# Own raw buffers for the weight steps with sums, and attention tables loaded once per layer

## The chip, the cores and the metric

The kernel runs on one core of a Trainium2 chip. The metric is the device time of one execution in microseconds (us), lower is better. The engines are named as in the profile: PE is TensorE (matrix products; PEld is its loading of weights), DVE is VectorE, ACT is ScalarE, POOL is GpSimd, and SP is SyncE, which here only issues transfers (DMAs).

## The reference

A two-layer encoder in float32 over 256 positions of width 2048. Cut to what matters:

```python
for l in range(2):
    h = rms_norm(x, attn_norm[l])
    proj = h @ w_in[l]
    ...
    mixed = jnp.concatenate([out_a, out_b, out_c], axis=-1)
    x = x + mixed @ w_o[l]
    h = rms_norm(x, mlp_norm[l])
    x = x + jnp.square(jax.nn.relu(h @ w_up[l])) @ w_down[l]
return rms_norm(x, final_norm)
```

`w_up[l]` is 2048x8192 and `w_down[l]` 8192x2048. The three mixers `out_a`, `out_b`, `out_c` are attention of three kinds; they need tables that do not depend on the input (cosines and sines of the rotary part, a mask, distances).

## The kernel before, in words

**Weights in two parts.** PE multiplies in a format with fewer bits than float32, so each weight tile is split: ACT casts the loaded raw tile to a high part (`wh`, line 132 or 147) and DVE subtracts that from the raw tile for a low part (`wl`, line 133 or 148). Activations are split in the same way, and each product is three matmuls (high by high, high by low, low by high).

**Stages.** A prologue loads `x` and the first weights and makes the statistic of the first norm: squares on POOL, line 252, added up in `acc`, line 253. Then comes, per layer, an attention phase and an MLP phase, which use the same region of on-chip memory one after the other: a pool is opened with the phase, `here["pool"]`. Other pools hold for the whole program: `cp` (x, gains, the tables `cn`, which are 128x1408 and hold the 128x128 identity `ident` in their first 128 columns, and others), `wp` (weights), `tp` (small work tiles, among them the rings `t1k` and `s2k` of three buffers each).

**MLP.** A layer's MLP takes four quarters of the hidden width; each quarter has two up products (names u00, u01, u10, ... quarter and half) and two down products (d00, d01, ...), so a layer has 16 products, and the program 32. `Product` (lines 281 to 353) computes one. It has 8 steps. A step loads two raw halves of 128x1024 (512 KB each, line 310, on SP's queue) and splits them. Steps 1, 2, 4, 5 and 7 are **plain**: two `wh`, two `wl`, 24 matmuls of 128x512. Steps 0, 3 and 6 are **steps with sums**: they save matmuls by working with sums of blocks of the weight. DVE forms the sums in place in the raw halves (lines 324 to 327), and these are split a second time into `th` and `tl` (ACT and DVE, two buffers each in the phase's pool). So a raw half of a plain step is free after its `wl`, one of a step with sums only after its `tl`: the second half (`raw[1]`) after the `tl` with the ending _2, the first (`raw[0]`) after that with the ending _3. After step 6 the results are put together on DVE (lines 346 to 350, `c`), after step 7 the last addition follows (line 352). An up product then goes through relu (ACT, line 771) and 16 transposes on PE (line 361) to a square (line 775); a down product's results are transposed and added to `x` by DVE (line 791).

All weights of the kernel, of plain steps and of steps with sums, go through one ring of four raw buffers:

```python
def rawt(name):
    return wp.tile([P, HW], F32, tag="raw", name=name, bufs=4)
```

`wh` and `wl` have five buffers each. A transfer into a buffer is issued when what the buffer held has been read for the last time. SP issues in the order that the program has for it, so an issue that waits holds up all behind it.

**What sets the order.** The framework simulates the program when it is built and orders each engine's instructions; tiles get their buffers in that order. There are no due times by hand.

The tables are loaded once, in the prologue, by `load_consts` (lines 119 to 121): `cn` and then `lm`, the vectors of the learned lambda, of which DVE makes `lamp` and `lams` (lines 442 to 449).

Of the kernel before, what the change touches and what calls it, by code (L numbers as in the profile page):

```python
# [10 lines left out]
F32 = mybir.dt.float32  # L11
# [5 lines left out]
P = 128  # L17
D = 2048
T = 256
DEPTH = 2  # L20
# [8 lines left out]
HW = 1024  # L29
# [7 lines left out]
def hybrid_encoder(ctx: ExitStack, tc: tile.TileContext, xT, wA, wQ, wKV, wB, wC, wO, wU, wD,  # L37
# [25 lines left out]
        return next(units(name, shape))  # L63

    def t1k(name):
        return tp.tile([P, T], F32, tag="t1k", name=name, bufs=3)

    def s2k(name):
        return tp.tile([P, 2, T], F32, tag="s2k", name=name, bufs=3)
# [31 lines left out]
    xp = [cp.tile([P, 2, T], F32, tag=f"x{k}", name=f"x{k}") for k in range(KT // 2)]  # L101
    x = [xp[k // 2][:, k % 2, :] for k in range(KT)]
    gn = cp.tile([P, G_END], F32, tag="gn", name="gn")
    cn = cp.tile([P, C_END], F32, tag="cn", name="cn")
    lm = tp.tile([P, DEPTH * 4 * 64], F32, tag="s2k", name="lm", bufs=3)
    ones = cp.tile([P, P], F32, tag="ones", name="ones")
    mhalf = cp.tile([P, 8], F32, tag="mhalf", name="mhalf")
# [2 lines left out]
    nc.gpsimd.memset(mhalf, -0.5)  # L110
    ones_r = cp.tile([P, P], F32R, tag="ones_r", name="ones_r")
    nc.scalar.copy(ones_r, ones)
    ident = cn[:, C_ID:C_ID + P]
    cosT = cn[:, C_COS:C_COS + T]
    sinT = cn[:, C_SIN:C_SIN + T]
    maskA = cn[:, C_MASK:C_MASK + 384]
    dist = cn[:, C_DIST:C_DIST + 384]

    def load_consts():
        nc.sync.dma_start(cn, consts)  # L120
        nc.sync.dma_start(lm, lams.to_broadcast([P, DEPTH * 4 * 64]))


    def weights(src, name, steps=(HW, HW)):
# [109 lines left out]
    class Stat:  # L234
# [7 lines left out]
        def add(self, xt):  # L242
            self.n += 1
            if self.n == 1:
                nc.gpsimd.tensor_tensor(self.acc, xt, xt, op=ALU.mult)  # L245
                return
            s = t1k(f"sq_{self.name}_{self.n}")
            if self.n == KT:
                nc.scalar.activation(s, xt, AF.Square)
                self.last = [s]  # L250
            else:
                nc.gpsimd.tensor_tensor(s, xt, xt, op=ALU.mult)
                nc.gpsimd.tensor_tensor(self.acc, self.acc, s, op=ALU.add)
# [27 lines left out]
    class Product:  # L281
# [22 lines left out]
        def step(self, i):  # L304
            nm = f"{self.name}_{i}"
            a = self.acts[i]
            a11, a12, a21, a22 = ((a[:, k, 0, HALF[t]], a[:, k, 1, HALF[t]]) for t in range(2) for k in range(2))
            raw = [rawt(f"raw_{nm}_{c}") for c in range(2)]
            for c in range(2):
                nc.sync.dma_start(raw[c], self.src[i][:, HW * c:HW * c + HW])  # L310
            if self.sums[i] is None:
                for c in range(2):
                    w = self.parts(raw[c], f"{nm}_{c}")
                    for b, aa in (("p2", (a11, a12)), ("p4", (a21, a22))) if c == 0 else (("p3", (a11, a12)), ("e", (a21, a22))):
                        for k in range(2):
                            self.add(b, aa[k], w[k])
                return
            s1, s2, s3, s4 = ((self.sums[i][:, 0, j], self.sums[i][:, 1, j]) for j in range(4))
            (b11, b21), (b12, b22) = ((r[:, 0:512], r[:, 512:]) for r in raw)
            w11, w21 = self.parts(raw[0], f"{nm}_0")  # L320
            self.add("p1", a11, w11)
            w22, = self.parts(b22, f"{nm}_1", 512)

            nc.vector.tensor_tensor(b22, b22, b12, op=ALU.subtract)
            nc.vector.tensor_tensor(b12, b11, b12, op=ALU.subtract)
            nc.vector.tensor_tensor(b11, b22, b11, op=ALU.add)
            nc.vector.tensor_tensor(b21, b21, b11, op=ALU.subtract)  # L327
            w1, w3 = self.parts(raw[1], f"{nm}_2", sums=True)
            self.add("p5", s1, w1)
            self.add("p7", s3, w3)  # L330
            w2, w4 = self.parts(raw[0], f"{nm}_3", sums=True)
            self.add("p6", s2, w2)
            self.add("p2", a12, w21)
            self.add("p3", s4, w22)
            self.add("p4", a22, w4)
# [97 lines left out]
    for i in range(1, 8):  # L433
        load_x(2 * i)
        first.step(i)
    load_consts()
    lam = []
    for l in range(DEPTH):
        pr = t1k(f"lamp{l}")[:, 0:128].rearrange("p (a b) -> p a b", a=2)
        for j in range(2):  # L440
            b0 = (l * 4 + 2 * j) * 64
            nc.vector.tensor_tensor(pr[:, j, :], lm[:, b0:b0 + 64], lm[:, b0 + 64:b0 + 128], op=ALU.mult)
        sm = cp.tile([P, 2], F32, tag=f"lams{l}", name=f"lams{l}")
        nc.vector.reduce_sum(sm, pr, axis=AX.X)
        ex = cp.tile([P, 2], F32, tag=f"lame{l}", name=f"lame{l}")
        nc.scalar.activation(ex, sm, AF.Exp)
        la = cp.tile([P, 1], F32, tag=f"lam{l}", name=f"lam{l}")
        init = 0.8 - 0.6 * math.exp(-0.3 * l)
        nc.vector.scalar_tensor_tensor(la, ex[:, 0:1], init, ex[:, 1:2], op0=ALU.add, op1=ALU.subtract)
        lam.append(la)  # L450

    for l in range(DEPTH):
        with phase(f"attention_{l}"):
            init = 0.8 - 0.6 * math.exp(-0.3 * l)
            if l > 0:
                first = Block(wA[l], xg, f"cq_{l}")
                for i in range(8):
                    first.step(i)
            r1 = stat.done()
            R1 = broadcast_sb(r1, 0, f"n1_{l}")  # L460

# [300 lines left out]
        with phase(f"mlp_{l}"):  # L762

            for qt in range(4):
# [43 lines left out]
                                                 scale=gn[:, G_FIN + i:G_FIN + i + 1])  # L808
                if last:
                    rf = broadcast(stat.done(), 0, "fin")[:, 0, :]  # L810
                    rs = t1k("rf")
                    nc.scalar.copy(rs, rf)
                    for n in (4, 0, 5, 1, 6, 2, 7, 3):
                        f = fin[n // 2][:, n % 2]
# [112 lines left out]
```

## Time and profile before

| | |
|---|---|
| time, median of 3 runs | 2177.9 us (2173.32 to 2182.52) |
| time of the profiled execution | 2177.18 us |
| span of its trace | 2175.1 us |
| granted PE clock over the span | 0.99 of full speed |
| busy PE, PEld | 2085.8, 1703.9 us |
| busy DVE, ACT, POOL | 1789.7, 1211.4, 199.4 us |
| loads of MLP weights | 512 of 512 KB |

The span is the time from the first to the last instruction of the trace; 2.1 us lie around it. Busy times are sums over instructions of an engine. Matmuls are pipelined and their ends are modelled, so PE that reads as busy can still be fed late; what PE waited for is read better from PEld. "Idle before, releaser" names what ended an engine's idle time.

### The profile page before, as it was taken

To read this page: it belongs to the slowest core of one execution; us is meant where nothing else is said; L and a number is where in the kernel's file an instruction comes from. 1 tells how busy PE (TensorE), PEld (TensorE's weight loads), DVE (VectorE), ACT (ScalarE), POOL (GpSimd) and SP (SyncE) were. 2 spreads that over 40 slices of the span, in tenths; PEclk is the share of its full clock that TensorE was granted. 3 is DMA by queue.
4 is the path that set the end of the run, shared out by engine and by line. 5 is a ranking of instruction groups with operands and counts; after the bars stand their busy time and mean duration, and the time that the engine had idled before them with its cause. 6 is when DMAs were issued, how large, how long until landed. Compare 5 with 4: busy or idle time off the path is not lost.

```text
span 2175.1 us, 28125 instructions
## 1 busy us (share of the span) xinstructions
PE 2085.8 (96%) x10138; PEld 1703.9 (78%) x10138; DVE 1789.7 (82%) x2572; ACT 1211.4 (56%) x1726; POOL 199.4 (9%) x256
## 2 busy tenths in 40 slices
PE   8999999999999999999899999999999999999997
PEld 6888888777777777777688888877777777777775
DVE  7767698988888888898886777988789878888986
ACT  5666645644654564465456665556446546644653
POOL 5101140000000000000221012300000000000021
PEclk9999999999999999999999999999999999999998
DMA  6535454555555555555555454555555555645553
GB/s 234 188 126 165 141 194 156 191 176 183 185 181 167 172 196 173 195 175 174 171 163 182 129 165 137 181 189 182 188 174 175 172 184 174 199 165 189 166 183 117
DMA packets 106267, 378.25 MB, mean 174 GB/s; under 512 B 11920, under 2 KB 13200, under 8 KB 106128
## 3 DMA queue, kind: packets, MB, share of 16 engines
q1 hardware_dynamic: 104832, 374.85, 52.4%
q8 instruction: 79, 1.29, 0.2%
q10 hardware_dynamic: 1296, 1.62, 0.2%
q14 instruction: 60, 0.49, 0.1%
HBM read 374.32 MB, written 2.10 MB: 173 GB/s over the span
## 4 chain that ended last, share of the span: by engine, by line
DVE 33%; PE 31%; DMA 21%; issue 7%; ACT 5%; POOL 2%; ACTq 0%; SPq 0%; DVEq 0%; POOLq 0%
DMA raw_u<-in_wU_dram 11%; DMA raw_d<-in_wD_dram 9%; DVE wl_d L148 5%; DVE wl_u L148 5%; PE p_d L296 4%; PE ps_wo L157 3%; DVE tl_u L148 3%; ACT wh_u L147 2%; DVE tl_d L148 2%; ACT wh_d L147 2%; PE ps_wo L158 2%; PE p_u L296 2%; DVE x L791 1%; PE ps_qC L157 1%; DVE c_u L352 1%
## 5 line engine op out<-in xcount | busy, mean ns | idle before, releaser
L147 ACT CAST wh_u<-raw_u 128x1024 fp32r<-128x1024 f32 (+1 forms) x256 | 248.2, 969 | 289.8 <-DMA raw_u<-in_wU_dram 262.6
L147 ACT CAST wh_d<-raw_d 128x1024 fp32r<-128x1024 f32 (+1 forms) x256 | 248.3, 970 | 287.4 <-DMA raw_d<-in_wD_dram 250.1
L296 PE MATMUL p_d<-wh_d,h_u 128*128 128x512 f32 x1152 | 392.4, 394 | 0.0
L296 PE MATMUL p_u<-wh_u,xm 128*128 128x512 f32 x1152 | 389.5, 392 | 0.0
L148 DVE TENSOR_TENSOR wl_d<-raw_d,wh_d 128x1024 fp32r<-128x1024 f32 (+1 forms) x256 | 288.0, 1139 | 102.6 <-ACT wh_d L147 102.0
L148 DVE TENSOR_TENSOR wl_u<-raw_u,wh_u 128x1024 fp32r<-128x1024 f32 (+1 forms) x256 | 285.7, 1127 | 101.5 <-ACT wh_u L147 100.9
L296 PEld LDWEIGHTS p_d<-wh_d,h_u 128*128 128x128 f32 x1152 | 218.0, 189 | 44.1
L296 PEld LDWEIGHTS p_u<-wh_u,xm 128*128 128x128 f32 x1152 | 216.8, 188 | 44.2
L296 PE MATMUL p_d<-wl_d,h_u 128*128 128x512 f32 x576 | 226.0, 392 | 0.1
L296 PE MATMUL p_u<-wl_u,xm 128*128 128x512 f32 x576 | 225.0, 391 | 0.0
L147 ACT CAST th_d<-raw_d 128x1024 fp32r<-128x1024 f32 x96 | 100.8, 1052 | 51.1 <-DVE raw_d L327 38.0
L245 POOL TENSOR_TENSOR acc_a<-x 128x256 f32<-128x256 f32 x2 | 1.2, 612 | 1389.2 <-DVE x L791 1389.2
L296 PEld LDWEIGHTS p_d<-wl_d,h_u 128*128 128x128 f32 x576 | 108.8, 189 | 23.4 <-DVE wl_d L148 1.0
L296 PEld LDWEIGHTS p_u<-wl_u,xm 128*128 128x128 f32 x576 | 108.2, 188 | 22.3
L296 PE MATMUL p_d<-th_d,s_h_u 128*128 128x512 f32 x288 | 109.9, 421 | 12.3 <-ACT th_d L147 12.2
L147 ACT CAST th_u<-raw_u 128x1024 fp32r<-128x1024 f32 x96 | 100.7, 1049 | 35.9 <-DVE raw_u L327 22.3
L148 DVE TENSOR_TENSOR tl_d<-raw_d,th_d 128x1024 fp32r<-128x1024 f32 x96 | 116.7, 1238 | 0.0
L148 DVE TENSOR_TENSOR tl_u<-raw_u,th_u 128x1024 fp32r<-128x1024 f32 x96 | 116.6, 1230 | 0.0
L296 PE MATMUL e_d<-wh_d,h_u 128*128 128x512 f32 x320 | 111.5, 389 | 0.0
L296 PE MATMUL e_u<-wh_u,xm 128*128 128x512 f32 x320 | 111.5, 389 | 0.0
L296 PE MATMUL p_u<-th_u,s_xm 128*128 128x512 f32 x288 | 106.6, 411 | 2.7 <-ACT th_u L147 2.4
L133 DVE TENSOR_TENSOR wl_wo<-raw_wo,wh_wo 128x1024 fp32r<-128x1024 f32 x64 | 86.2, 1349 | 20.5 <-ACT wh_wo L132 20.0
(451 smaller groups left out, 4764.7 us busy)
## 6 DMA issues: line engine op xcount, KB each, us to landing
raw_u<-in_wU_dram SPq DMA_DIRECT2D x256, 512.0 KB, 4.8
raw_d<-in_wD_dram SPq DMA_DIRECT2D x256, 512.0 KB, 5.0
raw_wo<-in_wO_dram SPq DMA_DIRECT2D x64, 512.0 KB, 3.7
raw_qB<-in_wB_dram SPq DMA_DIRECT2D x16, 512.0 KB, 4.2
raw_kB<-in_wB_dram SPq DMA_DIRECT2D x16, 512.0 KB, 3.7
raw_vB<-in_wB_dram SPq DMA_DIRECT2D x16, 512.0 KB, 4.4
raw_qC<-in_wC_dram SPq DMA_DIRECT2D x16, 512.0 KB, 3.5
raw_kC<-in_wC_dram SPq DMA_DIRECT2D x16, 512.0 KB, 3.4
```

Of the source, the lines that this page charges most:

```text
L133: nc.vector.tensor_tensor(wl[:, :n], raw[:, :n], as32(wh[:, :n]), op=ALU.subtract)
L147: nc.scalar.copy(h, src)
L148: (eng or nc.vector).tensor_tensor(l, src, as32(h), op=ALU.subtract)
L157: nc.tensor.matmul(ps, wh, a, start=i == 0, stop=False)
L158: nc.tensor.matmul(ps[:, 1, :], wl, a[:, 0, :], start=False, stop=i == n - 1)
L245: nc.gpsimd.tensor_tensor(self.acc, xt, xt, op=ALU.mult)
L296: nc.tensor.matmul(self.ps[b], x, y, start=self.n[b] == 1, stop=self.n[b] == self.total[b])
L352: nc.vector.tensor_tensor(c, self.ps[b], c, op=ALU.add)
L791: nc.vector.tensor_tensor(xp[n], turned(cs, f, nm), xp[n], op=ALU.add)
```

## The change

It does three things. The raw halves of steps with sums come from a ring of their own, `rs`, of three buffers in the phase's pool, so that the ring of four is left to plain steps and attention. To make place, the tables are no longer resident: `cn` loses the identity, which gets a tile and a load of its own, and becomes a tile of the attention phase's pool that is loaded in each layer (640 KB), in layer 0 on SP's queue and in layer 1 on POOL's. And `t1k` moves into the phase's pool, while those of its users that live between phases (the squares `sq`, `lamp`, the last `rf`) move to the ring `s2k`.

```diff
     def t1k(name):
-        return tp.tile([P, T], F32, tag="t1k", name=name, bufs=3)
+        return here["pool"].tile([P, T], F32, tag="t1k", name=name, bufs=3)
...
-    cn = cp.tile([P, C_END], F32, tag="cn", name="cn")
+    ident = cp.tile([P, P], F32, tag="ident", name="ident")
     lm = tp.tile([P, DEPTH * 4 * 64], F32, tag="s2k", name="lm", bufs=3)
...
-    ident = cn[:, C_ID:C_ID + P]
...
-    def load_consts():
-        nc.sync.dma_start(cn, consts)
-        nc.sync.dma_start(lm, lams.to_broadcast([P, DEPTH * 4 * 64]))
+    def load_consts(name, eng):
+        cn = here["pool"].tile([P, C_END - P], F32, tag="cn", name=name, bufs=1)
+        eng.dma_start(cn, consts[:, P:])
+        return [cn[:, c - P:c - P + n] for c, n in ((C_COS, T), (C_SIN, T), (C_MASK, 384), (C_DIST, 384))]
...
-            s = t1k(f"sq_{self.name}_{self.n}")
+            s = s2k(f"sq_{self.name}_{self.n}")[:, 0, :]
...
-            raw = [rawt(f"raw_{nm}_{c}") for c in range(2)]
+            raw = [rawt(f"raw_{nm}_{c}") if self.sums[i] is None else
+                   here["pool"].tile([P, HW], F32, tag="rs", name=f"rs_{nm}_{c}", bufs=3) for c in range(2)]
...
-    load_consts()
+    nc.sync.dma_start(ident, consts[:, 0:P])
+    nc.sync.dma_start(lm, lams.to_broadcast([P, DEPTH * 4 * 64]))
...
-        pr = t1k(f"lamp{l}")[:, 0:128].rearrange("p (a b) -> p a b", a=2)
+        pr = s2k(f"lamp{l}")[:, 0, 0:128].rearrange("p (a b) -> p a b", a=2)
...
+            cosT, sinT, maskA, dist = load_consts(f"cn_{l}", nc.sync if l == 0 else nc.gpsimd)
             r1 = stat.done()
...
-                    rs = t1k("rf")
+                    rs = s2k("rf")[:, 0, :]
```

**Place 1: SP at the start of product u20 of layer 0.** In a name like `raw_u20_0_3_1` stand the product, the layer, the step and the half; the number at the end is only a serial number. Before:

```order
L310 DMA raw_u20_0_0_0_6672<-in_wU_dram 128x1024
L310 DMA raw_u20_0_0_1_6673<-in_wU_dram 128x1024
L310 DMA raw_u20_0_1_0_6724<-in_wU_dram 128x1024
L310 DMA raw_u20_0_1_1_6725<-in_wU_dram 128x1024
L310 DMA raw_u20_0_2_0_6761<-in_wU_dram 128x1024
L310 DMA raw_u20_0_2_1_6762<-in_wU_dram 128x1024
L310 DMA raw_u20_0_3_0_6797<-in_wU_dram 128x1024
L310 DMA raw_u20_0_3_1_6798<-in_wU_dram 128x1024
L310 DMA raw_u20_0_4_0_6842<-in_wU_dram 128x1024
L310 DMA raw_u20_0_4_1_6843<-in_wU_dram 128x1024
L310 DMA raw_u20_0_5_0_6878<-in_wU_dram 128x1024
```

And with the change, from the first of these halves on:

```order
L308 DMA rs_u20_0_0_0_6674<-in_wU_dram 128x1024
L308 DMA raw_u20_0_1_0_6726<-in_wU_dram 128x1024
L308 DMA raw_u20_0_1_1_6727<-in_wU_dram 128x1024
L308 DMA raw_u20_0_2_0_6763<-in_wU_dram 128x1024
L308 DMA rs_u20_0_0_1_6675<-in_wU_dram 128x1024
L308 DMA rs_u20_0_3_0_6799<-in_wU_dram 128x1024
L308 DMA raw_u20_0_2_1_6764<-in_wU_dram 128x1024
L308 DMA rs_u20_0_3_1_6800<-in_wU_dram 128x1024
L308 DMA rs_u20_0_6_0_6916<-in_wU_dram 128x1024
L308 DMA raw_u20_0_4_0_6844<-in_wU_dram 128x1024
L308 DMA raw_u20_0_4_1_6845<-in_wU_dram 128x1024
L308 DMA raw_u20_0_5_0_6880<-in_wU_dram 128x1024
```

Three plain halves now stand ahead of the second half of step 0, and the first half of step 3 right behind it; the halves of step 6 stand as far ahead as their ring of three lets them.

**Place 2: DVE in step 3 of product u21 of layer 0.** `wl` are low parts of raw halves, `tl` those of sums. Before:

```order
L148 TENSOR_TENSOR wl_u21_0_3_0_7196<-raw_u21_0_3_0_7191,wh_u21_0_3_0_7195 128x1024
L148 TENSOR_TENSOR wl_u21_0_3_1_7203<-raw_u21_0_3_1_7192,wh_u21_0_3_1_7202 128x512
L324 TENSOR_TENSOR raw_u21_0_3_1_7192<-raw_u21_0_3_1_7192 128x512
L148 TENSOR_TENSOR wl_u21_0_4_0_7241<-raw_u21_0_4_0_7236,wh_u21_0_4_0_7240 128x1024
L325 TENSOR_TENSOR raw_u21_0_3_1_7192<-raw_u21_0_3_0_7191,raw_u21_0_3_1_7192 128x512
L148 TENSOR_TENSOR wl_u21_0_4_1_7257<-raw_u21_0_4_1_7237,wh_u21_0_4_1_7256 128x1024
L326 TENSOR_TENSOR raw_u21_0_3_0_7191<-raw_u21_0_3_1_7192,raw_u21_0_3_0_7191 128x512
L148 TENSOR_TENSOR tl_u21_0_3_2_7211<-raw_u21_0_3_1_7192,th_u21_0_3_2_7210 128x1024
L327 TENSOR_TENSOR raw_u21_0_3_0_7191<-raw_u21_0_3_0_7191 128x512
L148 TENSOR_TENSOR wl_u21_0_5_0_7277<-raw_u21_0_5_0_7272,wh_u21_0_5_0_7276 128x1024
L148 TENSOR_TENSOR tl_u21_0_3_3_7221<-raw_u21_0_3_0_7191,th_u21_0_3_3_7220 128x1024
```

With the change:

```order
L145 TENSOR_TENSOR wl_u21_0_3_0_7198<-rs_u21_0_3_0_7193,wh_u21_0_3_0_7197 128x1024
L145 TENSOR_TENSOR wl_u21_0_3_1_7205<-rs_u21_0_3_1_7194,wh_u21_0_3_1_7204 128x512
L145 TENSOR_TENSOR wl_u21_0_4_0_7243<-raw_u21_0_4_0_7238,wh_u21_0_4_0_7242 128x1024
L322 TENSOR_TENSOR rs_u21_0_3_1_7194<-rs_u21_0_3_1_7194 128x512
L145 TENSOR_TENSOR wl_u21_0_4_1_7259<-raw_u21_0_4_1_7239,wh_u21_0_4_1_7258 128x1024
L323 TENSOR_TENSOR rs_u21_0_3_1_7194<-rs_u21_0_3_0_7193,rs_u21_0_3_1_7194 128x512
L324 TENSOR_TENSOR rs_u21_0_3_0_7193<-rs_u21_0_3_1_7194,rs_u21_0_3_0_7193 128x512
L325 TENSOR_TENSOR rs_u21_0_3_0_7193<-rs_u21_0_3_0_7193 128x512
L145 TENSOR_TENSOR wl_u21_0_5_0_7279<-raw_u21_0_5_0_7274,wh_u21_0_5_0_7278 128x1024
L145 TENSOR_TENSOR tl_u21_0_3_2_7213<-rs_u21_0_3_1_7194,th_u21_0_3_2_7212 128x1024
L145 TENSOR_TENSOR tl_u21_0_3_3_7223<-rs_u21_0_3_0_7193,th_u21_0_3_3_7222 128x1024
```

The same eleven operations stand there. The low part of step 5's first half has gone ahead of the first `tl`, and those of step 4 stand further ahead among the sums. In most other products DVE's order is as it was.

**Place 3: SP in the prologue.** What an issue waits for stands in brackets: a name with Pool is a count of POOL's instructions, DVE one of DVE's, DMAHW an earlier transfer. Before:

```order
L131 DMA raw_cq_0_7_0_350<-in_wA_dram 128x1024 [waits DMAHW2_49,DVE_49]
L120 DMA cn_82<-in_consts_dram 128x1408 [waits DMAHW3_49]
L121 DMA lm_83<-in_lams_dram 128x512 [waits DMAHW4_49]
L131 DMA raw_kr_0_0_498<-in_wA_dram 128x1024 [waits DMAHW5_49,DVE_49]
L131 DMA raw_kr_0_1024_504<-in_wA_dram 128x1024 [waits DMAHW6_49,DVE_49]
L131 DMA raw_qB0_0_0_561<-in_wB_dram 128x1024 [waits DMAHW7_49,DMAHW0_49,DVE_49]
L131 DMA raw_qB0_0_1024_567<-in_wB_dram 128x1024 [waits DMAHW2_49,DVE_49]
```

With the change:

```order
L128 DMA raw_cq_0_7_0_350<-in_wA_dram 128x1024 [waits DMAHW2_49,DVE_49]
L434 DMA ident_82<-in_consts_dram 128x128 [waits DMAHW3_49]
L117 DMA cn_0_395<-in_consts_dram 128x1280 [waits DMAHW4_49]
L435 DMA lm_83<-in_lams_dram 128x512 [waits DMAHW5_49,Pool_49]
L128 DMA raw_kr_0_0_500<-in_wA_dram 128x1024 [waits DMAHW6_49,DVE_49]
L128 DMA raw_kr_0_1024_506<-in_wA_dram 128x1024 [waits DMAHW7_49,DVE_49]
L128 DMA raw_qB0_0_0_563<-in_wB_dram 128x1024 [waits DMAHW0_49,DVE_49]
L128 DMA raw_qB0_0_1024_569<-in_wB_dram 128x1024 [waits DMAHW2_49,DMAHW1_49,DVE_49]
```

`lm` now waits for POOL as well: its buffer in the ring `s2k` held square 14 of the statistic of `x`, and the count of POOL's instructions that it waits for is reached with the addition that reads this square (line 253). The loads behind it on SP, of `raw_kr` and `raw_qB`, come after it. On POOL one row is added, the load of the tables in layer 1, between the additions of squares 8 and 9 of that layer's statistic.

## Rows read from the trace of the kernel before

**Rows 1.** The page, part 1: busy us, share of the span, instructions.

```profile
PE 2085.8 (96%) x10138; PEld 1703.9 (78%) x10138; DVE 1789.7 (82%) x2572; ACT 1211.4 (56%) x1726; POOL 199.4 (9%) x256
```

**Rows 2.** The page, part 4: shares of the chain that ended last, by engine.

```profile
DVE 33%; PE 31%; DMA 21%; issue 7%; ACT 5%; POOL 2%; ACTq 0%; SPq 0%; DVEq 0%; POOLq 0%
```

**Rows 3.** Stretches (stages): from:to, length; busy us (instructions) per engine; clock, DMA share, GB/s.

```profile
320.00:1085.00 765.00, 731.91 (x3243) 581.42 (x3243) 655.80 (x815) 416.99 (x493) 21.39 (x20) 0.99 0.54 178
...
1395.00:2150.00 755.00, 725.35 (x3221) 577.19 (x3220) 647.50 (x803) 413.55 (x489) 23.19 (x20) 1.00 0.53 177
```

**Rows 4.** Stretches: single products of layer 0 (u00, u01, u20), and all fifteen.

```profile
334.50:377.90 43.40, 43.30 (x198) 35.47 (x196) 36.06 (x45) 22.69 (x26) 0.71 (x1) 1.00 0.58 193
377.90:424.70 46.80, 45.53 (x200) 35.24 (x199) 41.60 (x57) 29.18 (x38) 0.00 (x0) 1.00 0.55 180
...
707.40:755.50 48.10, 44.94 (x202) 35.73 (x201) 39.42 (x48) 23.13 (x25) 0.00 (x0) 1.00 0.53 175
...
sum 699.60, PE 673.29 PEld 534.65 DVE 599.48 ACT 386.05 POOL 0.71; mean PE 44.89 PEld 35.64 DVE 39.97 ACT 25.74 POOL 0.05
```

**Rows 5.** PEld's waits over the span: us in total, times, longest.

```profile
PEld t_u L361 <- ACT c_u L771: 27.2, 41, 1.5
PEld p_d L296 <- ACT th_d L147: 24.3, 33, 1.8
PEld p_u L296 <- DVE tl_u L148: 22.3, 34, 1.4
PEld p_d L296 <- DVE tl_d L148: 20.7, 18, 4.1
PEld t_d L361 <- DVE c_d L352: 19.4, 30, 1.1
PEld p_u L296 <- ACT th_u L147: 14.5, 32, 1.0
```

**Rows 6.** DVE's waits over the span.

```profile
DVE wl_d L148 <- ACT wh_d L147: 102.0, 92, 2.5
DVE wl_u L148 <- ACT wh_u L147: 100.9, 102, 2.5
```

**Rows 7.** Chain of waits, start of product u20: start us, us, what.

```profile
695.04 5.68 DMA raw_u<-in_wU_dram
...
713.99 6.10 DMA raw_u<-in_wU_dram
```

**Rows 8.** Timeline of DVE there: start us, us, operation [idle before <-releaser].

```profile
708.07 2.48 DVE L791 TENSOR_TENSOR x<-t_d,x 128x512 f32<-128x512 f32 x4
...
712.73 2.36 DVE L148 TENSOR_TENSOR wl_u<-raw_u,wh_u 128x1024 fp32r<-128x1024 f32 x2
716.20 1.23 DVE L148 TENSOR_TENSOR wl_u<-raw_u,wh_u 128x1024 fp32r<-128x1024 f32 x1 [1.11 <-ACT wh_u L147]
718.97 1.23 DVE L148 TENSOR_TENSOR wl_u<-raw_u,wh_u 128x1024 fp32r<-128x1024 f32 x1 [1.54 <-ACT wh_u L147]
```

**Rows 9.** Timeline of PEld in the same product.

```profile
725.74 0.30 PEld L296 LDWEIGHTS p_u<-th_u,s_xm 128*128 128x128 f32 x2 [0.70 <-ACT th_u L147]
727.47 0.19 PEld L296 LDWEIGHTS p_u<-tl_u,s_xm 128*128 128x128 f32 x1 [1.44 <-DVE tl_u L148]
```

**Rows 10.** The page, part 6: KB each, median us from issue to landing.

```profile
raw_d<-in_wD_dram SPq DMA_DIRECT2D x256, 512.0 KB, 5.0
```

**Rows 11.** Timeline of SP in the prologue.

```profile
18.82 0.43 SPq L121 DMA_DIRECT2D lm<-in_lams_dram  x1
```

**Rows 12.** Timeline of POOL in the prologue.

```profile
30.38 1.52 POOL L253 TENSOR_TENSOR acc_x<-acc_x,sq_x 128x256 f32<-128x256 f32 x2
```

**Rows 13.** Timeline of PE after the prologue.

```profile
40.21 0.77 PE L157 MATMUL ps_kr<-xg_a,wh_kr 128*128 128x512 f32 x1
```

**Rows 14.** Timeline of POOL at the start of attention in layer 1.

```profile
1101.09 1.62 POOL L253 TENSOR_TENSOR acc_a<-acc_a,sq_a 128x256 f32<-128x256 f32 x2
1114.66 0.71 POOL L210 TENSOR_TENSOR r_a<-v_a,mhalf 128x2 f32<-128x2 f32 x1 [11.96 <-DVE v_a L207]
```

More of the change, by code (lines that the diff above doesn't have):

```diff
@@ L112, in hybrid_encoder @@
     nc.scalar.copy(ones_r, ones)
-    ident = cn[:, C_ID:C_ID + P]
[L114 to L117, printed above, removed]
-    def load_consts():
-        nc.sync.dma_start(cn, consts)
-        nc.sync.dma_start(lm, lams.to_broadcast([P, DEPTH * 4 * 64]))
+    def load_consts(name, eng):
+        cn = here["pool"].tile([P, C_END - P], F32, tag="cn", name=name, bufs=1)
+        eng.dma_start(cn, consts[:, P:])
+        return [cn[:, c - P:c - P + n] for c, n in ((C_COS, T), (C_SIN, T), (C_MASK, 384), (C_DIST, 384))]
     def weights(src, name, steps=(HW, HW)):
```

## The prediction

> **What bounds the kernel now.** I read the busy shares first [rows 1]. PE is busy for 2085.8 of 2175.1 us, so it leaves little; but its matmuls overlap and their ends are modelled, so a late feed hides in that figure, and PEld (78%) and DVE (82%) have room. The chain of waits [rows 2] runs through DVE, PE and DMA to 33, 31 and 21%: a loop in which each waits for the next in turn, and no engine that is full. The stretches say where: the two MLP stretches are 765 + 755 = 1520 us long, of which PE is busy for 731.9 + 725.4 = 1457.3 [rows 3]. The attention stretches hold no step with sums, and I leave them alone.
>
> Inside an MLP the unit is the product. Fifteen of them in layer 0 took 699.60 us together, 699.60 / 15 = 46.64 each; the first, u00, whose weights could be loaded ahead, took 43.40 [rows 4]. So about 3.2 us of each later product is not PE's work. What PE's weight loads wait for [rows 5] has two kinds. For `th` and `tl`, the parts of the sums, they wait 24.3 + 22.3 + 20.7 + 14.5 = 81.8 us in 33 + 34 + 18 + 32 = 117 waits; for the results to be transposed at a product's end 27.2 + 19.4 = 46.6 us in 71.
>
> Why are the sums late? DVE makes them, and DVE waits 102.0 + 100.9 = 202.9 us for `wh` [rows 6], nearly all of its idle 1520 - 655.8 - 647.5 = 216.7 us in the MLP stretches [rows 3]. ACT, at 56% [rows 1], casts as soon as a load lands, so that wait is a load's. The start of product u20 shows it. A load could be issued only at 695.04, when a `tl` of the product before gave its buffer free, and took 5.68 us [rows 7]. Then DVE does the sums, the last operations of the product before and four additions to `x`, until 708.07 + 2.48 [rows 8], with the ring of four held all the while by steps 0 and 1. The next load that the chain shows, of step 3, is issued at 713.99 and takes 6.10 us [rows 7], and DVE waits 1.11 and 1.54 us for casts of step 2 at 716.20 and 718.97 [rows 8]. At step 3 PE then waits 0.70 us for a `th` and 1.44 us for a `tl` [rows 9]: 2.1 us in one product.
>
> **The change, part by part.** The sum is made against the profiled execution, 2177.18 us, of which 2175.1 are the span; it is 0.7 us under the median of the runs.
>
> *The ring of three for sums.* By the order of SP the halves now take turns so: the second half of step 3 takes the buffer of step 0's second half (free after `tl` _2 of step 0), the first of step 6 that of step 0's first (after `tl` _3), the second of step 6 that of step 3's second, the next product's step 0 those of step 3's first and step 6's second, its step 3's first that of step 6's first. The four plain buffers no longer wait for any `tl`. So at the start of a product steps 1 and 2 and the first half of step 3 are on chip or on the way before the sums of step 0 begin. Left is step 3's second half. From `tl` _2 of step 0 to its use DVE has one `tl` and five `wl`, 6 x 1.18 = 7.1 us (half of the pair at 712.73 [rows 8]); the load takes 5.0 us in the median [rows 10], up to 6.10 [rows 7], and its cast one more. It lands just in time. DVE from there to the first `tl` of step 3: five `wl`, 5.9 us, half a one, 0.6, four sums of 0.62 (a quarter of 2.48 [rows 8]), 2.5, one `tl`, 1.2, together 10.2 us; PE has the 48 matmuls of steps 1 and 2 and the nine of step 3 that need no sum, 57 x 43.40 / 198 = 12.5 us [rows 4]. So DVE is 2.3 us ahead where it was late, and the waits at steps 3 and 6 go.
>
> Step 0 is another matter: its second half still waits for `tl` _2 of the step 6 before it, as the load at 695.04 did [rows 7], and DVE does the ends of one product before the sums of the next. I let one wait per product stay, at the mean of the cheapest kind, 14.5 / 32 = 0.45 us [rows 5]: 32 x 0.45 = 14.4. The term is -(81.8 - 14.4) = **-67.4 us**; its ends are -40.9 (half of the waits) and -81.8 (all).
>
> *Transposes.* The change does not move them, and PE must end a product before DVE can finish its result. But DVE comes to that place earlier when it has not waited for loads, above all in down products. Of the 19.4 us there [rows 5] I take **-8**; ends 0 and -19.4. The 27.2 us of up products, where ACT's relu lies between, I leave.
>
> *Order in the second up and down products.* One `wl` goes ahead of a `tl` at step 3 (place 2): 1.2 us of the 2.3 ahead; PE has a further step to multiply before it needs that `tl`. Nothing, as long as the lead lasts; without it some 1.2 us in half the products, 19 us, inside the bounds above.
>
> *`lm` behind POOL.* Before, it was issued at 18.82 [rows 11]. Now it needs POOL's addition of square 14; the pair of additions at 30.38 ends at 31.90 [rows 12]. SP stands for up to 31.90 - 18.82 = 13.1 us, and behind it stand `raw_kr` and `raw_qB` (place 3). But the first matmul on `raw_kr` came only at 40.21 [rows 13]: from 31.90 there are 8.3 us for a load of 5.0, a cast and a `wl` of 1.2 each, 7.4 in all, if nothing else is on the way; yet `lm` itself lies ahead, and DVE's `lamp` waits for it ahead of that `wl`. I take **+2 us**, near the row of the matmul; ends 0 and +13.1. A gain is excluded: the same bytes of tables still go ahead of these loads.
>
> *Tables in layer 1.* The new load is issued by POOL among the squares, the last of which are added by 1101.09 + 1.62; POOL then stood idle for 11.96 us until 1114.66 [rows 14], and every use of the tables lies behind the norm that this makes. 640 KB at the rate of 512 KB in 5.0 us [rows 10] is 6.3 us. Nothing; without the cover, 6.3 us once.
>
> By the Trainium skill (DMA: Bandwidth & Descriptors, Anatomy of one DMA, SWDGE path) a transfer issued by POOL takes 2.0 us and its bytes over 436 GB/s: an estimate of 3.5 us for this one, and the sum would be the same; no run here shows such a load.
>
> *Squares in `s2k`, `t1k` in the phase's pool, the identity by itself.* POOL is busy for 9% [rows 1] and adds its squares in order, so three buffers serve as well in either ring: nothing.
>
> The sum: 2177.2 - 67.4 - 8 + 2 = **2103.8 us**, 44.3 us per product (46.64 - 75.4 / 32). DVE's 39.97 us per product, at most some 41.6 [rows 4], fit below that, and so do the loads: 16 x 512 KB in 44.3 us are 189 GB/s, and u00's stretch moved 193 [rows 4].
>
> **The rivals.** *DVE takes the place of the loads.* Its idle time is needed at a product's end, where it must wait for PE and the transposes, and what it gains before it loses there; the sums stay late half of the time. For it: 41.60 of 46.80 us in u01 is the fullest engine beside PE [rows 4]. Against it: 202.9 us of waits on loads [rows 6]. Half of the 75.4 goes: 2177.2 - 37.7 + 2 = 2141.5 us. Chance 0.17.
>
> The Trainium skill (Perfetto Trace Analysis, Identifying the Most-Contended Engine) says to judge PE by its weight loads rather than its matmuls and to work first on the engine with the highest occupancy. By that rule it is DVE here, 82% against 78%, whose work this change leaves as it is, and little would be won; the timeline, where DVE waits for loads at the place in question, speaks against it.
>
> *More goes than the sums.* DVE is far enough ahead for all of the 81.8 and half of the 46.6 us: 2177.2 - 81.8 - 23.3 + 2 = 2074 us. For it: u00 ran in 43.40 [rows 4]. Against: each transposed tile must still come from the engine before. Chance 0.10.
>
> *The wait moves to the ring of three.* Each second half of a step with sums still waits for a `tl`. If it lands after DVE is there, by 2 us or more in each of steps 0, 3 and 6, PE waits as now: within 11 us of 2177. Against it: the 7.1 us against 6 above. Chance 0.06.
>
> *Slower: the prologue pays and the MLP gains nothing.* SP's 13.1 us behind `lm` reach PE in full if the loads queued there land one by one at 5 to 6 us and PE runs dry; with the MLP as it is, 2177.2 + 13.1 = 2190 us. It decides if the first matmul on `raw_kr` comes later than about 51. Chance 0.06.
>
> **How the numbers follow.** The forecast has 0.61. Its own range is 2177.2 - 55 + 13 = 2135 to 2177.2 - 81.8 - 19.4 = 2076. The range that holds the time 8 times in 10 leaves out the last two rivals and the outer edges: 2074 to 2145 us. Half a per cent, 11 us, is about what a measurement of this kernel tells from no change. Faster by more than that: 0.61 + 0.17 + 0.10 = 0.88; the same 0.06; slower 0.06.
>
> **What would show it.** Right: products of 44 to 45 us in the stretches after the first; DVE's waits for `wh` at most half of 202.9 us; PEld's waits for `th` and `tl` near 14 us; those for transposes hardly changed; SP idle before `lm` until about 32, the first matmul on `raw_kr` at 40 to 45. Wrong: PEld's waits for sums above 40 us; DVE waiting for `wh` of a second half in steps 3 or 6 (late ring of three); SP or PE in attention of layer 1 waiting for the tables.

## The result, and the profile after

The change takes 2098.81 us in the median of four runs (2097.47 to 2103.65); the kernel before, run beside it, 2179.02. The ratio is 0.9638, with a 95% interval of 0.9612 to 0.9665: 3.6% faster, some 79 us. The forecast was 2103.8 us. The profiled execution took 2098.85 us.

The busy shares of the change, and below them its chain of waits by engine, against [rows 1, 2]:

```profile
PE 2050.8 (98%) x10138; PEld 1704.6 (81%) x10138; DVE 1786.9 (85%) x2572; ACT 1192.7 (57%) x1726; POOL 202.7 (10%) x257
...
PE 72%; DVE 14%; DMA 7%; ACT 4%; issue 2%; POOL 2%; SPq 0%; ACTq 0%; DVEq 0%; POOLq 0%
```

PE, DVE and ACT execute as many instructions as before and POOL one more, but the chain has changed its owner: PE has 72% of it where DVE, PE and DMA took turns at 33, 31 and 21%. The stretches of the change (from:to, length, busy us of PE, PEld, DVE, ACT, POOL, then the granted clock, the DMA share and GB/s):

```profile
37.00:322.00 285.00, 280.94 (x1663) 245.05 (x1662) 214.22 (x445) 175.56 (x349) 55.23 (x82) 0.99 0.54 174
322.00:1046.00 724.00, 714.61 (x3242) 582.99 (x3242) 656.36 (x817) 407.64 (x494) 22.89 (x21) 1.00 0.57 186
1046.00:1356.00 310.00, 307.27 (x1823) 267.43 (x1822) 232.34 (x460) 184.57 (x362) 67.43 (x96) 1.00 0.53 170
1356.00:2072.00 716.00, 708.80 (x3215) 577.51 (x3214) 647.28 (x802) 404.32 (x489) 25.43 (x20) 1.00 0.56 184
```

The two MLP stretches went from 765 and 755 us [rows 3] to 724 and 716: 41 + 39 = 80 us. The first MLP begins 2 us later than at 320, and the second attention stretch is 310 us as before. So the whole gain lies in the MLPs. Single products of layer 0 (u00, u01, u20, u21) and the sum of the fifteen, against [rows 4]:

```profile
336.30:379.90 43.60, 43.41 (x197) 35.41 (x197) 36.52 (x45) 21.70 (x27) 1.63 (x1) 1.00 0.58 193
379.90:425.20 45.30, 44.42 (x203) 35.64 (x201) 41.26 (x57) 28.26 (x37) 0.00 (x0) 1.00 0.58 186
...
689.70:733.00 43.30, 43.30 (x202) 35.98 (x200) 39.04 (x48) 22.44 (x26) 0.00 (x0) 1.00 0.60 195
733.00:778.00 45.00, 44.27 (x200) 35.50 (x199) 41.13 (x57) 28.09 (x37) 0.00 (x0) 1.00 0.60 187
...
sum 661.30, PE 657.43 PEld 536.86 DVE 598.58 ACT 377.08 POOL 1.63; mean PE 43.83 PEld 35.79 DVE 39.91 ACT 25.14 POOL 0.11
```

661.30 / 15 = 44.09 us per product in place of 46.64, and u20 runs in 43.30 with PE busy throughout. What PEld waits for, against [rows 5]:

```profile
PEld t_u L359 <- ACT c_u L771: 12.1, 18, 1.5
PEld p_d L293 <- DVE tl_d L145: 9.8, 9, 3.0
PEld p_u L293 <- ACT th_u L144: 6.8, 24, 0.4
...
PEld p_u L293 <- DVE tl_u L145: 5.8, 15, 0.8
...
PEld p_d L293 <- ACT th_d L144: 2.7, 9, 0.3
```

For `th` and `tl` it is 9.8 + 6.8 + 5.8 + 2.7 = 25.1 us, from 81.8; for results to be transposed 12.1 us, from 46.6: the row of the down products (`t_d`, 19.4 us) is gone. DVE's waits for casts, against [rows 6], fell from 202.9 to 112.1 us:

```profile
DVE wl_u L145 <- ACT wh_u L144: 61.6, 52, 3.8
DVE wl_d L145 <- ACT wh_d L144: 50.5, 47, 2.2
```

The chain of waits at the start of u20, where [rows 7] had two loads of 5.68 and 6.10 us, is now PE's work alone (start us, us, what):

```profile
687.66 1.37 PE e_d L293 x6
689.02 0.88 PE t_d L359 x8
...
691.24 8.42 PE p_u L293 x37
```

### The profile page after: what moved, and what is told of

Same layout as the page of the kernel before. It is cut to its first block, busy times and chain, and to the rows that moved or that the text cites. A ratio compares the mean times of both kernels' runs of the same rounds, so it can differ in the third digit from the quotient of the medians.

```text
span 2097.1 us, 28040 instructions
## 1 busy us (share of the span) xinstructions
PE 2050.8 (98%) x10138; PEld 1704.6 (81%) x10138; DVE 1786.9 (85%) x2572; ACT 1192.7 (57%) x1726; POOL 202.7 (10%) x257
## 4 chain that ended last, share of the span: by engine, by line
PE 72%; DVE 14%; DMA 7%; ACT 4%; issue 2%; POOL 2%; SPq 0%; ACTq 0%; DVEq 0%; POOLq 0%
PE p_d L293 22%; PE p_u L293 15%; PE e_d L293 4%; PE ps_wo L154 4%; PE e_u L293 3%; DVE wl_u L145 2%; DMA rs_u<-in_wU_dram 2%; PE ps_wo L155 2%; DMA rs_d<-in_wD_dram 2%; DVE tl_u L145 2%; PE ps_qC L154 1%; PE ps_kC L154 1%; PE ps_kB L154 1%; PE ps_qB L154 1%; PE t_u L359 1%
## 5 line engine op out<-in xcount | busy, mean ns | idle before, releaser
L144 ACT CAST wh_d<-raw_d 128x1024 fp32r<-128x1024 f32 x160 | 168.1, 1051 | 134.6 <-PE e_d L293 46.3
L144 ACT CAST wh_u<-raw_u 128x1024 fp32r<-128x1024 f32 x160 | 168.3, 1052 | 125.2 <-PE e_u L293 46.0
L145 DVE TENSOR_TENSOR wl_u<-raw_u,wh_u 128x1024 fp32r<-128x1024 f32 x160 | 193.4, 1218 | 19.8 <-ACT wh_u L144 19.0
L145 DVE TENSOR_TENSOR wl_d<-raw_d,wh_d 128x1024 fp32r<-128x1024 f32 x160 | 196.5, 1244 | 16.0 <-ACT wh_d L144 15.2
L144 ACT CAST wh_d<-rs_d 128x1024 fp32r<-128x1024 f32 x96 | 80.3, 837 | 138.4 <-PE p_d L293 78.2
L145 DVE TENSOR_TENSOR wl_u<-rs_u,wh_u 128x1024 fp32r<-128x1024 f32 x96 | 91.1, 961 | 42.7 <-ACT wh_u L144 42.6
L145 DVE TENSOR_TENSOR wl_d<-rs_d,wh_d 128x1024 fp32r<-128x1024 f32 x96 | 91.2, 963 | 35.5 <-ACT wh_d L144 35.3
L145 DVE TENSOR_TENSOR tl_d<-rs_d,th_d 128x1024 fp32r<-128x1024 f32 x96 | 116.6, 1235 | 0.3
L145 DVE TENSOR_TENSOR tl_u<-rs_u,th_u 128x1024 fp32r<-128x1024 f32 x96 | 115.1, 1226 | 0.3
L144 ACT CAST th_u<-rs_u 128x1024 fp32r<-128x1024 f32 x96 | 98.9, 1048 | 18.7 <-DVE rs_u L325 11.5
```

Source lines behind the costliest of these rows:

```text
L144: nc.scalar.copy(h, src)
L145: (eng or nc.vector).tensor_tensor(l, src, as32(h), op=ALU.subtract)
```

## The experiments

The theory was that of the prediction: plain halves no longer wait for a `tl`, so loads lie ahead. Rivals: only the number of raw buffers counts (seven for four); DVE is the bound; other parts of the change do it.

**The ring taken back.** In the change, with all the rest left:

```diff
-            raw = [rawt(f"raw_{nm}_{c}") if self.sums[i] is None else
-                   here["pool"].tile([P, HW], F32, tag="rs", name=f"rs_{nm}_{c}", bufs=3) for c in range(2)]
+            raw = [rawt(f"raw_{nm}_{c}") for c in range(2)]
```

> The change with its ring of three taken back: the halves of steps with sums come again from the ring of four; tables per layer, squares, t1k and lm stay as changed. Theory (the ring of three is the whole gain, the other parts cost 0 to 2 us): 2177 to 2183 us, products of 46.6 us, and PEld waits for th and tl near 82 us. Rival (part of the gain comes from the other parts, such as less traffic or another order): 2110 to 2165 us.

2178.41 us, ratio to before 0.9998 (0.9982 to 1.0013). PEld waits 82.2 us for `th` and `tl`. The theory holds in both figures. Tables, squares, `t1k`, the identity and `lm` together cost nothing that can be measured, and the ring is the whole gain.

**Seven buffers, shared out by halves.**

```diff
-            raw = [rawt(f"raw_{nm}_{c}") if self.sums[i] is None else
+            raw = [rawt(f"raw_{nm}_{c}") if c == 0 else
```

> Seven raw buffers as in the change, four and three, but shared out by halves: first halves of every step from the ring of four, second halves of every step from the ring of three. The orders on PE, DVE, ACT and POOL are those of the change; only SP's differs. Theory (what counts is that plain halves do not stand behind a tl): second halves of steps 1 and 2 wait again for a tl of the step 0 or the step 6 before, and some of the stalls come back, 2115 to 2150 us. Rival (what counts is the number of buffers, four against seven): within 5 us of the change, 2094 to 2104 us.

2084.38 us, ratio 0.9568 (0.9550 to 0.9586): 14 us faster than the change. The instructions on PE, DVE, ACT and POOL stand in the same order as in the change; only SP's loads do not. Both the theory (2115 to 2150) and the rival (2094 to 2104) are off: sums and plain halves behind one another do no harm, they do good. Single products of this run, u00, u21 and u20:

```profile
334.40:377.90 43.50, 43.27 (x196) 35.40 (x195) 36.44 (x45) 21.61 (x27) 1.62 (x1) 1.00 0.55 193
726.50:770.50 44.00, 44.00 (x202) 35.76 (x201) 41.75 (x57) 28.76 (x38) 0.00 (x0) 1.00 0.60 191
683.30:726.50 43.20, 43.20 (x201) 35.99 (x200) 38.96 (x47) 22.47 (x26) 0.00 (x0) 1.00 0.60 195
```

u21 takes 44.0 us here, 45.0 in the change (the row before the sum, above). The place is DVE's first operation on the second half of step 6. The timeline of DVE, first of the change, then of this run:

```profile
760.94 0.69 DVE L145 TENSOR_TENSOR wl_u<-rs_u,wh_u 128x512 fp32r<-128x512 f32 x1 [3.29 <-ACT wh_u L144]
```

```profile
752.50 0.69 DVE L145 TENSOR_TENSOR wl_u<-rs_u,wh_u 128x512 fp32r<-128x512 f32 x1 [1.24 <-ACT wh_u L144]
```

In the change DVE stood 3.29 us there and came late to the end of the product, where PE's transposes waited for it; the 12.1 us of `t_u` waits have no row any more in the mixed run. The orders of the two programs say why. In the change this half takes the buffer of step 3's second half, free only after a `tl`; in the mixed run it takes, in u21, that of step 4's second half, free after a `wl`. Its issue on SP's queue and its cast on ACT, first of the change, then of the mixed run:

```profile
754.27 0.33 SPq L308 DMA_DIRECT2D rs_u<-in_wU_dram  x1
...
760.29 0.62 ACT L144 CAST wh_u<-rs_u 128x512 fp32r<-128x512 f32 x1 [5.11 <-DMA rs_u<-in_wU_dram]
```

```profile
743.55 0.33 SPq L308 DMA_DIRECT2D rs_u<-in_wU_dram  x1
...
751.84 0.62 ACT L144 CAST wh_u<-rs_u 128x512 fp32r<-128x512 f32 x1 [3.05 <-issue]
```

In the change the cast waits for the load; in the mixed run it does not, and what the 1.24 us are then for stays open. Over the whole span, DVE's idle time ahead of the splits `wl` of the second halves in steps with sums (the figure behind the second bar of each row; first the change, then the mixed run) goes from 67.7 to 51.9 us, 15.8 us less, for a gain of 14 us:

```profile
L145 DVE TENSOR_TENSOR wl_d<-rs_d,wh_d 128x512 fp32r<-128x512 f32 x48 | 33.5, 698 | 31.7 <-ACT wh_d L144 31.7
L145 DVE TENSOR_TENSOR wl_u<-rs_u,wh_u 128x512 fp32r<-128x512 f32 x48 | 32.9, 686 | 36.0 <-ACT wh_u L144 35.9
```

```profile
L145 DVE TENSOR_TENSOR wl_d<-rs_d,wh_d 128x512 fp32r<-128x512 f32 x48 | 33.5, 698 | 29.1 <-ACT wh_d L144 29.1
L145 DVE TENSOR_TENSOR wl_u<-rs_u,wh_u 128x512 fp32r<-128x512 f32 x48 | 33.0, 687 | 22.8 <-ACT wh_u L144 22.8
```

**Two buffers for the sums.**

```diff
-                   here["pool"].tile([P, HW], F32, tag="rs", name=f"rs_{nm}_{c}", bufs=3) for c in range(2)]
+                   here["pool"].tile([P, HW], F32, tag="rs", name=f"rs_{nm}_{c}", bufs=2) for c in range(2)]
```

> The change with two buffers in place of three in the ring for sums. Theory: the separation still holds for the plain halves, but the first half of step 3 can be loaded only after the last tl of step 0; from there DVE has 4 wl, 4.7 us, and a load and a cast take 6, so DVE loses 1.3 us of the 2 to 3 that it is ahead in each step 3 and 6: 2100 to 2120 us, PEld waits for th and tl 25 to 45 us (25.1 in the change). Rival (the number of buffers counts, six lie two thirds of the way from four to seven): about 2125 us. Rival (the third buffer is what does it): 2140 us or more.

2282.26 us, ratio 1.0479 (1.0457 to 1.0501): not 20 us slower than the change but 183, and 105 slower than before, with six buffers in place of four. The theory and the rival of the number fall. The third, 2140 us or more, holds, but it did not foresee a time above that of the kernel before. The chain of waits of this run, from the second half of step 3 of product d11 to step 0 of u20, shows why:

```profile
686.46 1.23 DVE tl_d L145
687.71 6.81 DMA rs_d<-in_wD_dram
694.62 0.63 ACT wh_d L144
695.27 0.70 DVE wl_d L145
...
703.08 1.23 DVE tl_d L145
704.33 5.98 DMA rs_d<-in_wD_dram
...
717.94 1.14 DVE tl_d L145
719.10 6.11 DMA rs_u<-in_wU_dram
```

A second half cannot be loaded before the last `tl` of the sums ahead of it, then takes 6 us to land, is cast, worked on and split, and its last `tl` lets the next one load. One such round took 704.33 - 687.71 = 16.6 us, the next 14.8. There are three in a product, some 47 us, more than PE's 43.3: the ring of two is a loop that is longer than the product, however many plain halves lie ready. My expectation had looked at the time from a `tl` to the next use only, and not at the whole round. (The order on PE and DVE also differs here from the change in part of its rows; how much of the 183 us that makes is open.)

**Mixed, with two for the second halves.** As the mixed rings, `bufs=2`.

> As the run with mixed rings (first halves of all steps from four buffers, second halves from the ring in the phase's pool: 2084.4 us), but with two buffers for the second halves: six in all. Theory after the first runs (what counts is how many transfers can be ahead of DVE at the worst place of a product, the step 6 followed by the next step 0, and that no buffer passes from sums straight to sums there): with two, the next step 0's second half takes the buffer of step 6's second half and waits for its tl, as in the kernel before; 2100 to 2140 us. Rival (any ring of two is too short whatever is in it, as in the run with a ring of two for sums, 2282 us): above 2178 us. Rival (six or seven buffers make no difference when mixed): 2080 to 2090 us.

2112.95 us, ratio 0.9689 (0.9672 to 0.9707): as the theory has it. Six buffers mixed are 0.079 of the time better than six kept apart, so a ring of two is not too short in itself.

**The rings swapped**: sums from the ring of four, plain halves from that of three.

```diff
-            raw = [rawt(f"raw_{nm}_{c}") if self.sums[i] is None else
+            raw = [rawt(f"raw_{nm}_{c}") if self.sums[i] is not None else
```

> The change with the rings swapped: halves of steps with sums from the ring of four, those of plain steps from the ring of three in the phase's pool. Theory (the sums' halves are held longest and are the ones that were late in steps 6 and 0, so four for them takes the boundary's wait away, since step 0 then takes the buffers of step 3): products end without a late DVE, but the ten plain halves have only three buffers and are loaded later: 2085 to 2110 us. Rival (plain halves are what must be ahead): 2120 us or more.

2115.55 us, ratio 0.9700 (0.9676 to 0.9724), between theory and rival. The transposes' waits are gone, as forecast, but now a plain half is late. DVE's timeline in product u20:

```profile
708.61 1.23 DVE L145 TENSOR_TENSOR wl_u<-rs_u,wh_u 128x1024 fp32r<-128x1024 f32 x1 [6.22 <-ACT wh_u L144]
```

**One ring of seven, in turn.**

```diff
-            raw = [rawt(f"raw_{nm}_{c}") if self.sums[i] is None else
-                   here["pool"].tile([P, HW], F32, tag="rs", name=f"rs_{nm}_{c}", bufs=3) for c in range(2)]
+            raw = []
+            for c in range(2):
+                turn[0] = (turn[0] + 1) % 7
+                raw.append(rawt(f"raw_{nm}_{c}") if turn[0] < 4 else
+                           here["pool"].tile([P, HW], F32, tag="rs", name=f"rs_{nm}_{c}", bufs=3))
```

> Seven raw buffers taken in turn by all halves of the MLP, as one ring (four from the common pool, three from the phase's). A half then takes the buffer of the one seven places ahead of it, so step 0's halves take those of step 4's second and step 5's first half, plain ones, and only halves of steps 3, 4, 6 and 7 follow halves of sums, 3.5 steps behind. Theory (depth counts, not separation): 2080 to 2086 us, as the mixed rings or a little better. Rival (mixing as such harms where the rings do not keep halves apart): 2095 us or more.

2093.79 us, ratio 0.9597 (0.9581 to 0.9613). That lies between the theory (up to 2086) and the rival (from 2095), and the measurement does not tell which is nearer. It is short of the mixed rings: depth is not all.

**Mixed the other way round**: second halves from four, first halves from three (`c == 1` for `c == 0`).

> The mixed rings the other way round: second halves of all steps from the ring of four, first halves from the ring of three; the orders on PE, DVE and ACT differ from those of the change in few rows. Theory (the halves that are late are the second ones of steps 3 and 6, and with four buffers they take those of plain steps: step 6's that of step 2): DVE's gap of 1.2 us before the second half of step 6 goes, 2078 to 2086 us. Rival (the first halves with three become late in their place, step 6's taking that of step 3): 2084 to 2095 us.

2112.10 us, ratio 0.9688 (0.9663 to 0.9713): slower than its mirror image by 28 us, beyond both expectations. In u20 the first half of step 3 takes, of the three, the buffer of step 0's first half, which is free only after the later `tl`, and DVE needs it before the second half. DVE's timeline there shows the gap:

```profile
702.51 1.23 DVE L145 TENSOR_TENSOR wl_u<-rs_u,wh_u 128x1024 fp32r<-128x1024 f32 x1 [3.84 <-ACT wh_u L144]
```

**`lm` on POOL's queue**, so that SP does not stand behind POOL's additions.

```diff
-    nc.sync.dma_start(lm, lams.to_broadcast([P, DEPTH * 4 * 64]))
+    nc.gpsimd.dma_start(lm, lams.to_broadcast([P, DEPTH * 4 * 64]))
```

> The change with lm loaded on POOL's queue, so that SP does not stand behind POOL's additions. Theory (the wait of lm costs the prologue 1 to 2 us): SP issues raw_kr near 22 us in place of 33.6, the first matmul of product u00 comes 1 to 2 us earlier than 336.3, time 2096 to 2099 us. Rival (the shift of 1.8 us in the prologue comes from before lm, or the order of the loads does not matter there): u00 at 336 to 337 us, no difference.

2101.77 us, ratio 0.9644 (0.9624 to 0.9665): no difference, as the rival has it. SP's last issue before `lm`, `lm` and the loads of `raw_kr`, and the first matmul on them, all of the change:

```profile
20.58 0.43 SPq L117 DMA_DIRECT2D cn<-in_consts_dram  x1
33.13 0.33 SPq L435 DMA_DIRECT2D lm<-in_lams_dram  x1
33.56 0.85 SPq L128 DMA_DIRECT2D raw_kr<-in_wA_dram  x2
...
39.97 0.50 PE L154 MATMUL ps_kr<-xg_a,wh_kr 128*128 128x512 f32 x1 [1.37 <-ACT wh_kr L129]
```

And with `lm` on POOL:

```profile
21.52 3.51 SPq L128 DMA_DIRECT2D raw_kr<-in_wA_dram  x2
...
41.13 0.80 PE L154 MATMUL ps_kr<-xg_a,wh_kr 128*128 128x512 f32 x1 [0.55 <-ACT wh_kr L129]
```

The loads go 12 us earlier and the matmul does not. The wait is real and costs nothing.

**Tables of layer 1 on SP** (`nc.sync` in both layers).

> The change with the tables of layer 1 loaded on SP in place of POOL; the orders on PE, DVE and ACT are those of the change. Theory (the load is hidden on either queue as long as what it waits for, the last sums of the layer's MLP, is done when SP comes to it): within 3 us of the change. Rival (SP stands behind it while loads of the next attention could go): 3 to 10 us slower, with PE idle for raw_cq after the end of MLP 0.

2096.58 us, ratio 0.9626 (0.9603 to 0.9648): the same, as the theory has it. Here the load is hidden on either queue.

**More work for DVE in the change.** In each plain step:

```diff
                     w = self.parts(raw[c], f"{nm}_{c}")
+                    if c == 0:
+                        nc.vector.tensor_tensor(w[0][1], raw[c][:, 0:512], as32(w[0][0]), op=ALU.subtract)
```

> The change with more work for DVE: in each plain step the first half of one wl (128x512, 0.6 us) is computed a second time, 5 x 0.6 = 3.0 us per product, 96 us in all, DVE 42.9 us of a product's 44.1. Theory (PE sets the time now and DVE has about 4 us to spare per product, but part of its lead at steps 0 and 3 goes): 10 to 35 us slower than the change, 2109 to 2134 us. Rival (DVE is the bound now): 60 to 96 us slower, 2159 to 2195 us.

2134.47 us, ratio 0.9803 (0.9783 to 0.9822): 36 us more than the change, at the upper edge of the theory and far from the rival's 60. The busy shares of this run:

```profile
PE 2068.4 (97%) x10138; PEld 1709.3 (80%) x10138; DVE 1874.9 (88%) x2732; ACT 1193.2 (56%) x1726; POOL 203.5 (10%) x257
```

DVE has 1874.9 - 1786.9 = 88 us more to do, of which 36 show. So DVE is near the bound now, but it is not the bound. (The order differs in some rows, too, and the granted clock of the span was 0.987 of full speed against 0.993 in the change; what part of the 36 us these make is not separated.)

**The same in the kernel before.**

> The same 96 us of work for DVE in the kernel before. Theory (there DVE stands in the loop of load, cast, wl, release, load, so each operation ahead of a release delays the next load): 30 to 70 us slower than before, 2209 to 2249 us, more than the same work costs in the change. Rival (DVE waits 203 us for loads, so its extra work falls into its idle time): under 15 us slower.

2308.10 us, ratio 1.0598 (1.0573 to 1.0624): 131 us more than before, above the theory's range. DVE's waits for casts:

```profile
DVE wl_d L148 <- ACT wh_d L147: 106.5, 101, 3.3
DVE wl_u L148 <- ACT wh_u L147: 103.6, 90, 3.7
```

They are 210.1 us, against 202.9 [rows 6], while DVE's busy time rose from 1789.7 [rows 1] to 1889.1 us: none of the 99 us fell into its idle time. Work and wait stand in series there, as the loop of load, cast, split, release and load wants it. That more than the work was added may come from the order, which differs in many rows, or from the granted clock, 0.980 in place of 0.991; it is not settled.

**Mixed rings and tables on SP.**

> Mixed rings (first halves four, second halves three) and the tables of layer 1 on SP: the best two single edits together. Theory (the two are independent and the second is worth 0 to 2 us): 2081 to 2086 us. Rival (POOL's load is free and SP's stands in the way): 2085 to 2090 us.

2083.26 us, ratio 0.9562 (0.9538 to 0.9586), as the mixed rings alone. Both beat the kernel before and the change.

All arrangements of the raw halves side by side (waits in us from the profiled executions, of the views shown above):

| raw halves | time, us | ratio to before | DVE for casts (MLP) | PEld for `th`, `tl` | PEld for `c` |
|---|---|---|---|---|---|
| plain 4, sums 2 | 2282.3 | 1.0479 | 270.4 | 138.9 | 57.3 |
| one ring of 4 (before) | 2179.0 | 1 | 202.9 | 81.8 | 46.6 |
| one ring of 4, tables moved | 2178.4 | 0.9998 | 197.3 | 82.2 | 44.5 |
| plain 3, sums 4 | 2115.6 | 0.9700 | 140.7 | 46.5 | 0 |
| first 4, second 2 | 2113.0 | 0.9689 | 120.3 | 46.4 | 4.0 |
| first 3, second 4 | 2112.1 | 0.9688 | 123.4 | 49.0 | 0 |
| plain 4, sums 3 (the change) | 2098.8 | 0.9638 | 112.1 | 25.1 | 12.1 |
| 7 in turn | 2093.8 | 0.9597 | 104.4 | 28.0 | 2.2 |
| first 4, second 3 | 2084.4 | 0.9568 | 94.9 | 21.3 | 0 |

DVE's waits fall with the time from row to row, except between 2113.0 and 2112.1 us, which the measurement does not tell apart. So the time goes with how long DVE stands for casts. Most of these waits stand behind a load, but not all, as the 1.24 us above show, and a microsecond of them has no fixed price: 90.8 us less gave 80 from the kernel before to the change, 158.3 us more cost 183 with the ring of two for the sums.

## Why the prediction was right

The time, 5 us off, lies well in the range, and the mechanism that carries the sum is the right one: without the ring nothing is gained, with it the waits of DVE for loads and of PE for sums shrink. That it came as near as 5 us is in part luck, since two terms were off in opposite ways. Step by step:

- *What bounds the kernel before.* Right. The run with more DVE work there adds that the loop had no slack for it, and the chain of the change has PE at 72%.
- *The waits for sums*, -67.4 us forecast: from 81.8 to 25.1, -56.7. I had let 14.4 us stay, at step 0; 25.1 stayed. The 24 waits for `th_u`, 0.28 us on the average, are small ones as I had let stay; the 9.8 us for `tl_d` in 9 waits, 3.0 at the longest, are not.
- *Transposes*, -8 forecast, -19.4 as the end: from 46.6 to 12.1, -34.5. This term was mis-sized. It went beyond its end because I left the 27.2 us of up products in place, as ACT's relu lies between; 15.1 us of these went too, and in the mixed rings the rest, so relu was not what they were for. That they were long because DVE came late to the additions fits with this and is not shown by itself.
- *The two together*: -91.2 us of waits, -75.4 forecast, and 80 us less in the MLP stretches. The sums gave 10.7 us less than forecast, the transposes 26.5 us more, and the waits were not worth their full length in time. A wait of PEld is not all lost time: the 0.70 us at 725.74 [rows 9] stand beside 0.28 us in the timeline of PE in the kernel before:

```profile
725.74 0.73 PE L296 MATMUL p_u<-th_u,s_xm 128*128 128x512 f32 x2 [0.28 <-ACT th_u L147]
```

- *Order in the second products*, nothing as long as the lead lasts, up to 19 us without it. Here the lead did not last: the gap of 3.29 us in u21 is at a half that waits for a `tl` which stands behind three `wl` (place 2), and u01 and u21 took 45.3 and 45.0 us where u20 took 43.3. The bound named the size; the value taken was too low.
- *`lm`*, +2: the MLP did begin 2 us later, but the run without that wait is no earlier in its first matmul on `raw_kr`, and the mixed run, whose `lm` waits as well, begins its first product at 334.40, as the kernel before did (334.50 [rows 4]). The reason was wrong, and no run shows a cost of the wait.
- *Tables in layer 1*, nothing: right. The load on POOL's queue, in the view of DMA issues, landed in 6.5 us (6.3 taken):

```profile
cn<-in_consts_dram POOLq DMA_DIRECT2D x1, 640.0 KB, 6.5
```

 The estimate of 3.5 us from the Trainium skill (DMA: Bandwidth & Descriptors, Anatomy of one DMA, SWDGE path) does not hold here, with three loads of 512 KB going on in the same stretch; the measurement decides.
- *The rivals.* DVE as the next bound: against it the 36 of 88 us. By the Trainium skill's rule (Perfetto Trace Analysis, Identifying the Most-Contended Engine) DVE, with 85%, is still the engine to work on first; the trace agrees in so far as part of its added work shows, and disagrees for the change itself, which won 3.6% without touching DVE's work. The Trainium skill's remark (Perfetto Trace Analysis, Optimization Strategy) that a gap which repeats can mean too few buffers is the one that this case bears out: 46.64 to 44.09 us per product.
- *Signs and range.* DVE's waits for casts were to fall to half of 202.9 us, 101.5, or less; they are 112.1. The waits for transposes were hardly to change; they fell by 34.5 us. A second half of step 6 that DVE stands for was named as a sign of being wrong, and u21 shows one: there the third rival, the wait that moves to the ring of three, has its part. The upper end of the forecast's own range, 2177.2 - 55 + 13, has a 55 that no term gives; with the ends of the terms, -40.9, 0 and +13.1, it is 2149 us. The result lies inside either.
- *What I had wrong behind the right number.* "The four plain buffers no longer wait for any `tl`" was given as the cause. Keeping the kinds apart is not it: the same seven buffers mixed by halves are 14 us faster, and two kept for the sums are 105 us slower than one ring of four. What the runs point to is the round of each buffer: which half takes it after which, and whether load, cast, work and release of all halves that pass through it fit into a product. In the change the second halves of the sums pass one buffer on to each other; their loads were issued, in the timeline of SP (the first transfer of each row), at

```profile
677.29 1.46 SPq L308 DMA_DIRECT2D rs_u<-in_wU_dram  x2
...
693.30 1.46 SPq L308 DMA_DIRECT2D rs_u<-in_wU_dram  x2
...
705.42 0.33 SPq L308 DMA_DIRECT2D rs_u<-in_wU_dram  x1
...
720.59 1.46 SPq L308 DMA_DIRECT2D rs_u<-in_wU_dram  x2
```

 for step 0, 3 and 6 of u20 and step 0 of u21: 720.59 - 677.29 = 43.30 us, as long as the product itself. A round that repeats with the product must be that long, so this does not tell how much there is to spare; but PE is busy throughout u20, so there the round fits, and in u21, where DVE's order puts a `tl` behind three `wl`, it no longer does. That an arrangement loses time at a half that comes late to DVE is shown, in one product each, by the gaps above for the change, the swapped rings and the mixed rings the other way round; that no other cause takes part in the order of the table is argued, not shown.

## What to carry to other kernels

When an engine waits a little in every round of a loop and the loads are short of buffers, count for each buffer the whole round: issue, landing, every operation until its release, times the number of tiles that pass through this buffer in a period. If that comes near the period, more buffers can help without any work being made faster. By these runs, do not give the tiles that stay longest a small ring of their own: where it can be had, let them follow ones that leave early, and put the fewest buffers where the need comes latest.

## What the runs showed that I had not expected

Six buffers can be slower than four: 1.0479 with two kept for the sums, 0.9689 with two for second halves. An issue that holds up SP's queue for 12 us (20.58 + 0.43 to 33.13, and `raw_kr` issued at 33.56 in place of 21.52) can cost nothing. And 99 us of work added to DVE, which was idle for 216.7 of 1520 us in the MLPs, cost 131.
